# Last chunk of the last MLP: the left half of its columns from seven block products

## The chip, the cores and the metric

The kernel runs on one core of a Trainium2 chip. The metric is the device time of one execution in microseconds (us); for a kernel it is the median of several executions. A core has a matrix engine (TensorE, PE in the profile; its weight loads are PEld), a vector engine (VectorE, DVE), a scalar engine (ScalarE, ACT), GpSimd (POOL) and a queue engine (SyncE, SP). Each engine works through its own instructions in a fixed order and waits on semaphores that the others raise. DMA transfers are issued from SP, ACT or POOL and run on 16 DMA engines that they share.

## What is computed

A trunk of two layers over 256 tokens of width 2048: a state-space mixer in layer 0, a dilated attention mixer in layer 1, an MLP with squared ReLU behind each, and one last RMS norm. Only the second MLP and the norm behind it matter here:

```
def sq_relu_mlp(h, w1, w2):
    a = jax.nn.relu(h @ w1)
    return (a * a) @ w2

x = x + sq_relu_mlp(rms_norm(x, norm_mlp[i]), mlp_w1[i], mlp_w2[i])    # i = 1, the last layer
return rms_norm(x, final_norm)
```

`w1` is 2048 x 8192 and `w2` 8192 x 2048, all in float32.

## The kernel before

**Precision.** TensorE multiplies float32 in a fast format with a shorter mantissa (`F32R`). Each operand is therefore split in two: a high part, and a low part that holds the rest. For a unit of weights (128 x 2048 floats, 1 MB) ACT makes `wh` by a copy (`nc.scalar.activation(wh..)` in `fetch`), and DVE makes `wl` by subtracting `wh` from the weights. A product is then three matmuls: high by high, high by low, low by high.

**The plan.** `unit_plan` lists all units of weights in the order in which they are used, and `fetch` emits load and split of each, ahead of use. Units are numbered by their place in this list. A unit lands in one of three buffers `raw0` to `raw2` and is split into one of three or four slots of `wh` and `wl`; a slot is free once the matmuls of its last user are done. Chunks of the MLP may use four slots (`chunked`), plain units three.

**The MLP.** The 8192 hidden columns are cut into eight chunks of 1024 (`FC`). For chunk c, eight units of `w1` (`U0` to `U7`) give the hidden values, kept transposed in `r` (128 x 8 x 256: eight blocks of 128 hidden columns by 256 tokens). The chunk's part of `w2` is 1024 x 2048: eight units, each 512 hidden rows (half q) by 512 output columns (block j).

Chunks 0 to 6 do their part of `w2` by a seven-product scheme for 2 x 2 blocks (`PRODUCTS`, `PUT`, `Chunk.combine`, `product`). Blocks are the two halves of the hidden rows, the two halves of the tokens, and two neighbouring output blocks; the pair j = 0, 1 is marked `a` (left half of the columns) and the pair j = 2, 3 `b`. Each product has 12 matmuls of 128 x 512. On the side of the hidden values, `combine` forms the sums `s5`, `s6`, `s3`, `s7` on DVE and splits them. On the side of the weights, the sums are built up in place in a buffer `Aa` (or `Ab`):

- product 1 uses the block as it is loaded by SP;
- products 5 and 6 use `Aa` after another block was added to it by a transfer that POOL issues (`nc.gpsimd.dma_start(.., accum_op=ALU.add)`), the adding transfer;
- product 4 uses the negated sum of all four blocks. The fourth block is in `raw` for product 2 anyway, and DVE adds it (L263).

Products 3 and 7 use a second buffer `Ba` in the same way. An adding transfer into `Aa` can start only when the split of the value that is in it is done. The buffer `Aa` of a chunk is the same storage as `raw2` (`tag = f"raw{raws.use(2)}"` in `fetch`).

In `CHUNK_ORDER` the products of chunk c stand between the `w1` units of chunk c + 1: `1a U0 1b U1 5a U2 5b 3a ...`. Between products 1a and 5a TensorE works on U0, 1b and U1.

**The last chunk (c = 7)** has no next chunk, and all its eight units are plain (`rows_unit`): for each j, two units of 24 matmuls each (four blocks of hidden rows, two halves of the tokens, three matmuls), so 192 matmuls. `Chunk.complete` splits the one part of `r` that the plain form needs besides. After each j, DVE adds the result to `x_res` (`add_residual`) and `done(j)` runs, which is `gained` here: ACT squares the finished columns for the norm, and POOL multiplies them by the norm's gain `fin`. `fin` is loaded in `gained(0)`, into the buffer of `Ba`. For j = 3 both units are used together. After the last matmul stands a tail: the residual, the squares, the root, the scaling and the eight transfers to the output.

**What sets the order.** A scheduler orders each engine's instructions. The matmuls of a product are held behind those before them by `issue_after(latest[0])`, and the splits of the MLP's units are held in the order of the plan (`issue_after(high[i - 1])`, `issue_after(low[i - 1])`).

Of the kernel before, what the change touches and what calls it, by code (L numbers as in the profile page):

```python
# [8 lines left out]
F32 = mybir.dt.float32  # L9
# [5 lines left out]
P = 128  # L15
S = 256
NH = S // P
D = 2048
# [19 lines left out]
FC = 8  # L38
# [49 lines left out]

PRODUCTS = {
# [12 lines left out]
def mlp_plan(layer):  # L102
    plan = [("w1", layer, 0, u) for u in range(8)]
    for c in range(FC):
        if c + 1 < FC:
            for item in CHUNK_ORDER:
                if item[0] == "U":
                    plan.append(("w1", layer, c + 1, int(item[1])))
                else:
                    plan.append(("w2", layer, c, item))  # L110
        else:
            plan += [("w2", layer, c, j, q) for j in range(4) for q in range(2)]
    return plan
# [3 lines left out]
def hybrid_trunk_kernel(ctx: ExitStack, tc: tile.TileContext, a: dict, out: bass.AP):  # L117
    nc = tc.nc
# [24 lines left out]
    def bank(name, among):  # L143
        k = banks_of.use(banks_of.peek(among))
        return psum.tile([P, 512], F32, tag=f"b{k}", name=name, bufs=1)
# [24 lines left out]
    plan = unit_plan()  # L170
# [3 lines left out]
    latest = [None]  # L174
# [47 lines left out]
    def fetch(i, ends=(16,)):  # L222

        src, n = source(plan[i])
        kind = plan[i][0]
# [24 lines left out]
        ready[i] = (wh, wl)  # L250
        for k0, k1 in zip((0, *ends), ends):
            c = slice(k0 * n // 16, k1 * n // 16)
            if how == "load":
                load[i] = nc.sync.dma_start(raw[:, c], src[:, c]).ins
            elif how == "add" or kind == "wq":
                nc.gpsimd.dma_start(raw[:, c], src[:, c], accum_op=ALU.add)
            with ExitStack() as order:
# [3 lines left out]
                if item and item[0] == "2":  # L261
                    a = sums_of["A" + item[1]]
                    nc.vector.tensor_tensor(a[:, c], a[:, c], raw[:, c], ALU.add)  # L263
# [58 lines left out]
    def rows_unit(banks, us, lhs, k0, nk, n, first, last):  # L322

        ws = [take(*u) for u in us]
        kn = nk * len(us)
        for m in range(NH):
            t = slice(m * P, (m + 1) * P)
            for i in range(kn):
                wh, wl = ws[i // nk]
                c = slice((i % nk) * n, (i % nk + 1) * n)  # L330
                st, sp = first and i == 0, last and i == kn - 1
                hi, lo = lhs(k0 + i, 0, t), lhs(k0 + i, 1, t)
                nc.tensor.matmul(banks[m][:, :n], hi, wh[:, c], start=st, stop=False)  # L333
                nc.tensor.matmul(banks[m][:, :n], hi, wl[:, c], start=False, stop=False)  # L334
                latest[0] = nc.tensor.matmul(banks[m][:, :n], lo, wh[:, c], start=False, stop=sp).ins  # L335
# [710 lines left out]
    def mlp(layer, pool, xn, done):  # L1046
# [7 lines left out]

# [86 lines left out]
        for c in range(FC - 1):  # L1141
            of = cur.combine()
            nxt = Chunk(c + 1)
            for item in CHUNK_ORDER:
# [8 lines left out]
                kept = key == "za"  # L1153
                first = item[0] in "15" or item[0] == "2" and not (kept and c > 0)
# [3 lines left out]
                if not kept or c == FC - 2:  # L1158
                    j += 2 * (item[1] == "b")
                    xc = x_res[:, m, j * 512:(j + 1) * 512]  # L1160
                    nc.vector.tensor_tensor(xc, xc, banks[key], op)
            cur = nxt

# [21 lines left out]
    with tc.tile_pool(name="mlp1", bufs=1) as pool:  # L1185
# [5 lines left out]
        def gained(j):  # L1191
            if j == 0:
                fin.append(pool.tile([P, D], F32, tag="Ba", name="fin", bufs=1))
                nc.scalar.dma_start(fin[0], a["final_norm"].to_broadcast([P, D]))
# [5 lines left out]
            if j == 2:  # L1200
                nc.vector.tensor_reduce(mean[:, :, 0], ssq[:, :, :3], AX.X, ALU.add)
                nc.vector.tensor_scalar(mean[:, :, 0], mean[:, :, 0], 1.0 / D, EPS, ALU.mult, ALU.add)
# [110 lines left out]
```

## Time and profile before

| | us |
|---|---|
| median of three executions | 2531.31 (2530.99 to 2532.34) |
| the profiled execution | 2528.85 |
| its span, first to last instruction | 2527.1 |
| TensorE's wait before it starts the last chunk | 0 |
| from the start of the last matmul (2517.61) to the span's end | 9.49 |

The profile's page gives the busy time of each engine and the chain of work that ended last. Its other views list single instructions in order of time (start, duration, engine, line, output <- inputs, and in brackets how long the engine sat idle before it and what ended that), busy time by stretches of time, waits, and the DMA transfers with the time from issue to landing. TensorE is busy for 99% of the span. A matmul of 128 x 512 is listed with some 0.39 us, but the next one starts 0.227 us later: they overlap, so counts are multiplied by the distance of their starts.

### The profile page before, as it was taken

The page shows a single profiled execution, that of the slowest core. Times are in us where ns is not written, and L with a number is a line of the kernel's source. Part 1 is how long each engine was busy: PE and PEld are TensorE (multiplying, and loading weights), DVE is VectorE, ACT ScalarE, POOL GpSimd, SP SyncE. Part 2 cuts the span into 40 slices and gives each one's busy share as a digit, 9 for nine tenths or more (in the row PEclk, how much of TensorE's full clock was granted, in tenths as well). Part 3 has the DMA queues.
Part 4 walks back from the last instruction along what each step waited for, and adds up shares of the span by engine and source line. Part 5 has one row for each costly group of instructions (what it writes and reads, how often), then busy time and mean ns, then how long its engine had stood idle before and what let it go on. Part 6 is the DMA issues. An engine that isn't in the chain of part 4 may idle for free.

```text
span 2527.1 us, 34394 instructions
## 1 busy us (share of the span) xinstructions
PE 2508.9 (99%) x13737; PEld 2162.8 (86%) x13737; DVE 2057.1 (81%) x2287; ACT 1598.3 (63%) x1990; POOL 125.8 (5%) x143
## 2 busy tenths in 40 slices
PE   9999999999999999999999999999999999999998
PEld 7888888888888888888888999999888888888887
DVE  7778889798788889988886677677668989889885
ACT  7777677677666666666656666566566666666664
POOL 0001000100000000000000000000000000000001
PEclk9999999999999999999999999999999999999999
DMA  8557777877787899888955554444568988898883
GB/s 299 212 196 188 244 225 243 242 227 218 246 245 245 254 253 265 249 248 250 269 185 178 171 178 167 163 163 163 179 220 230 266 248 251 254 264 255 252 239 136
DMA packets 83696, 567.43 MB, mean 225 GB/s; under 512 B 9296, under 2 KB 9936, under 8 KB 20048
## 3 DMA queue, kind: packets, MB, share of 16 engines
q1 hardware_dynamic: 65232, 441.50, 47.8%
q0 software_dynamic: 15552, 113.25, 23.2%
q10 hardware_dynamic: 2752, 10.49, 1.2%
q8 instruction: 108, 1.77, 0.3%
q14 instruction: 52, 0.43, 0.0%
HBM read 563.04 MB, written 2.16 MB: 224 GB/s over the span
## 4 chain that ended last, share of the span: by engine, by line
PE 92%; DVE 2%; ACT 2%; DMA 1%; issue 1%; POOL 0%; SPq 0%; ACTq 0%; POOLq 0%; DVEq 0%
PE h L298 28%; PE qk L298 11%; PE c L298 7%; PE pxb L1130 6%; PE pxa L1130 6%; PE pwb L1130 3%; PE pwa L1130 3%; PE z L335 2%; PE z L333 2%; PE z L334 2%; PE v L333 2%; PE v L334 2%; PE v L335 2%; PE pzb L1130 2%; PE pza L1130 2%; DVE wl L271 1%
## 5 line engine op out<-in xcount | busy, mean ns | idle before, releaser
L271 DVE TENSOR_TENSOR wl<-raw,wh 128x2048 fp32r<-128x2048 f32 (+4 forms) x368 | 796.6, 2167 | 267.2 <-ACT wh L270 265.8
L270 ACT ACTIVATE wh<-raw 128x2048 fp32r<-128x2048 f32 (+4 forms) x368 | 669.5, 1821 | 357.3 <-PE h L298 78.2
L298 PE MATMUL h<-xn,wh 128*128 128x512 f32 x2048 | 690.2, 393 | 0.0
L298 PE MATMUL h<-xn,wl 128*128 128x256 f32 x2048 | 556.0, 281 | 0.2 <-DVE wl L271 0.2
L298 PEld LDWEIGHTS h<-xn,wh 128*128 128x128 f32 x2048 | 376.5, 188 | 75.4
L298 PEld LDWEIGHTS h<-xn,wl 128*128 128x128 f32 x2048 | 385.3, 188 | 14.3 <-DVE wl L271 0.5
L298 PE MATMUL c<-xn,wh 128*128 128x512 f32 x768 | 262.5, 394 | 1.5 <-ACT wh L270 1.4
L298 PE MATMUL qk<-xn,wh 128*128 128x512 f32 x768 | 259.3, 393 | 0.0
L298 PE MATMUL c<-xn,wl 128*128 128x256 f32 x768 | 210.7, 283 | 0.8 <-DVE wl L271 0.8
L298 PE MATMUL qk<-xn,wl 128*128 128x256 f32 x768 | 209.4, 284 | 0.0
L298 PEld LDWEIGHTS c<-xn,wh 128*128 128x128 f32 x768 | 142.0, 188 | 32.7 <-ACT wh L270 3.9
L298 PEld LDWEIGHTS qk<-xn,wh 128*128 128x128 f32 x768 | 141.2, 188 | 28.6
L298 PEld LDWEIGHTS c<-xn,wl 128*128 128x128 f32 x768 | 143.8, 188 | 5.6 <-DVE wl L271 1.8
L298 PEld LDWEIGHTS qk<-xn,wl 128*128 128x128 f32 x768 | 141.5, 188 | 3.6 <-issue 1.2
L270 ACT ACTIVATE wh<-Ab 128x2048 fp32r<-128x2048 f32 x42 | 80.4, 1915 | 81.6 <-DMA Ab<-in_w 54.8
L271 DVE TENSOR_TENSOR wl<-Ab,wh 128x2048 fp32r<-128x2048 f32 x42 | 96.1, 2288 | 18.6 <-ACT wh L270 18.4
L270 ACT ACTIVATE wh<-Aa 128x2048 fp32r<-128x2048 f32 x42 | 80.3, 1913 | 40.5 <-DMA Aa<-in_w 34.0
L271 DVE TENSOR_TENSOR wl<-Aa,wh 128x2048 fp32r<-128x2048 f32 x42 | 96.1, 2287 | 11.6 <-ACT wh L270 11.6
L1079 ACT ACTIVATE r<-r 128x256 f32<-128x256 f32 x128 | 52.2, 411 | 78.2 <-DVE r L1078 78.2
L333 PE MATMUL z<-wh,xn 128*128 128x512 f32 x256 | 98.7, 392 | 2.4 <-DVE c_5t L319 2.4
L335 PE MATMUL z<-wh,xn 128*128 128x512 f32 x256 | 100.1, 392 | 0.0
L334 PE MATMUL z<-wl,xn 128*128 128x512 f32 x256 | 99.9, 390 | 0.0
(471 smaller groups left out, 4967.7 us busy)
## 6 DMA issues: line engine op xcount, KB each, us to landing
raw<-in_w SPq DMA_DIRECT2D x172, 1024.0 KB, 5.5
raw<-in_w_in SPq DMA_DIRECT2D x74, 1024.0 KB, 4.9
raw<-in_w_qk SPq DMA_DIRECT2D x48, 1024.0 KB, 4.9
Aa<-in_w POOLq DMA_DIRECT2D x28, 1024.0 KB, 9.8
Ab<-in_w POOLq DMA_DIRECT2D x28, 1024.0 KB, 10.1
raw<-in_w_v SPq DMA_DIRECT2D x32, 768.0 KB, 4.4
A<-in_w_out POOLq DMA_DIRECT2D x18, 1024.0 KB, 9.0
raw<-in_w_out SPq DMA_DIRECT2D x14, 1024.0 KB, 7.6
```

What stands on the lines that cost most here:

```text
L270: high[i] = nc.scalar.activation(wh[:, c], raw[:, c], AF.Copy).ins
L271: low[i] = nc.vector.tensor_tensor(wl[:, c], raw[:, c], wh[:, c].bitcast(F32), ALU.subtract).ins
L298: latest[0] = nc.tensor.matmul(ps[:, :n], (wh, wl)[part][:, kt * P:(kt + 1) * P], xs[:, kt, :, :].rearrange("p a t -> p (a t)")[:, :n], st ...
L333: nc.tensor.matmul(banks[m][:, :n], hi, wh[:, c], start=st, stop=False)
L334: nc.tensor.matmul(banks[m][:, :n], hi, wl[:, c], start=False, stop=False)
L335: latest[0] = nc.tensor.matmul(banks[m][:, :n], lo, wh[:, c], start=False, stop=sp).ins
L1079: nc.scalar.activation(t, t, AF.Square)
L1130: latest[0] = nc.tensor.matmul(ps, lhs(i, part), w[:, n], start=(first and i == 0 and part == 0 and w is wh), stop=(i == 3 and part == 1), ...
```

## The change

The last chunk of the last MLP gets an order of its own, `LAST_ORDER`. Its left half (j = 0 and 1) comes from the seven products, and its right half (j = 2 and 3) stays plain: `P0`, `P1` are the two units of j = 2, set among the products, and `p0`, `p1` those of j = 3, at the end. In this chunk the fourth block is added to `Aa` by an adding transfer in place of DVE (`whole`), which reads that block a second time. `rows_unit` gets `strict`, which holds the second half of the tokens behind the first for j = 3. The norm's gain is loaded with j = 2, into the buffer of `Ab`, and j = 0 and 1 are finished after product 4a. The first MLP keeps its last chunk.

```diff
+LAST_ORDER = "1a 5a P0 3a 6a P1 7a 2a 4a p0 p1".split()
...
+        elif layer == 0:
+            plan += [("w2", layer, c, j, q) for j in range(4) for q in range(2)]
         else:
-            plan += [("w2", layer, c, j, q) for j in range(4) for q in range(2)]
+            plan += [("w2", layer, c, 2 + (item[0] == "p"), int(item[1])) if item[0] in "Pp" else
+                     ("w2", layer, c, item) for item in LAST_ORDER]
...
+        whole = kind == "w2" and plan[i][2] == FC - 1
...
-            elif how == "add" or kind == "wq":
+            elif how == "add" or kind == "wq" or how == "sum" and whole:
                 nc.gpsimd.dma_start(raw[:, c], src[:, c], accum_op=ALU.add)
...
-                if item and item[0] == "2":
+                if item and item[0] == "2" and not whole:
                     a = sums_of["A" + item[1]]
                     nc.vector.tensor_tensor(a[:, c], a[:, c], raw[:, c], ALU.add)
...
+            with ExitStack() as order:
+                if strict and m:
+                    order.enter_context(tc.issue_after(latest[0]))
...
-        for c in range(FC - 1):
+        last = FC - 1 if layer == 0 else FC
+        for c in range(last):
             of = cur.combine()
-            nxt = Chunk(c + 1)
-            for item in CHUNK_ORDER:
+            nxt = Chunk(c + 1) if c + 1 < FC else cur.complete()
+            for item in CHUNK_ORDER if c + 1 < FC else LAST_ORDER:
+                if item == "P0":
+                    plain = [bank(f"d{layer}_{c}_2_{m}", (0, 1)) for m in range(NH)]
+                if item[0] == "P":
+                    q = int(item[1])
+                    in_order(lambda: rows_unit(plain, [("w2", layer, c, 2, q)], cur.plain, 4 * q, 4, 512,
+                                               q == 0, q == 1))
+                    if q:
+                        add_residual(plain, 2)
+                        done(2)
+                    continue
+                if item == "p0":
+                    plain = [bank(f"d{layer}_{c}_3_{m}", (0, 1, 6)) for m in range(NH)]
+                    in_order(lambda: rows_unit(plain, [("w2", layer, c, 3, q) for q in range(2)], cur.plain,
+                                               0, 4, 512, True, True, strict=True))
+                    add_residual(plain, 3)
+                    done(3)
...
+                if c == FC - 1 and item == "4a":
+                    done(0)
+                    done(1)
...
-            if j == 0:
-                fin.append(pool.tile([P, D], F32, tag="Ba", name="fin", bufs=1))
+            if j == 2:
+                fin.append(pool.tile([P, D], F32, tag="Ab", name="fin", bufs=1))
...
-            if j == 2:
+            if j == 1:
                 nc.vector.tensor_reduce(mean[:, :, 0], ssq[:, :, :3], AX.X, ALU.add)
```

The units of the last chunk are numbered 551 to 558 before, and 551 to 561 with the change: 551 is 1a, 552 is 5a, 553 P0, 554 3a, 555 6a, 556 P1, 557 7a, 558 2a, 559 4a, 560 p0, 561 p1. Buffers carry the number of the unit for which they were first filled, so `Aa551` is the one buffer of 1a, 5a, 6a and 4a.

SP's queue at the end of the program, its last loads. Before:

```order
L254 DMA raw548_21110<-in_w1 128x2048
L254 DMA raw549_21129<-in_w2 128x2048
L254 DMA raw551_21167<-in_w2 128x2048
L254 DMA raw552_21213<-in_w2 128x2048
L254 DMA raw553_21250<-in_w2 128x2048
L254 DMA raw554_21280<-in_w2 128x2048
L254 DMA raw555_21320<-in_w2 128x2048
L254 DMA raw556_21350<-in_w2 128x2048
L254 DMA raw557_21388<-in_w2 128x2048
L254 DMA raw558_21418<-in_w2 128x2048
```

With the change:

```order
L262 DMA Ba554_21271<-in_w2 128x2048
L262 DMA raw548_21110<-in_w1 128x2048
L262 DMA raw549_21129<-in_w2 128x2048
L262 DMA Aa551_21166<-in_w2 128x2048
L262 DMA raw553_21265<-in_w2 128x2048
L262 DMA raw556_21311<-in_w2 128x2048
L262 DMA raw558_21359<-in_w2 128x2048
L262 DMA raw561_21434<-in_w2 128x2048
L262 DMA raw560_21415<-in_w2 128x2048
```

Eight plain loads become seven, and the load of 560 (p0) is issued last, behind that of 561 (p1). By the order of use of the three buffers, 553 takes `raw0`, 556 `raw1`, 558 `raw0`, 560 `raw2` and 561 `raw1`; `raw2` is the storage that `Aa551` holds until 4a is split.

POOL's queue at the end, the adding transfers and the norm's products (`x_res<-x_res,fin`). Before:

```order
L256 DMA Aa529_20515<-in_w2 128x2048
L256 DMA Ab531_20580<-in_w2 128x2048
L256 DMA Ba536_20751<-in_w2 128x2048
L256 DMA Bb538_20817<-in_w2 128x2048
L1199 TENSOR_TENSOR x_res_69<-x_res_69,fin_21312 128x512 x6
```

With the change:

```order
L264 DMA Ba536_20751<-in_w2 128x2048
L264 DMA Bb538_20817<-in_w2 128x2048
L264 DMA Aa551_21166<-in_w2 128x2048 x2
L264 DMA Ba554_21271<-in_w2 128x2048
L264 DMA Aa551_21166<-in_w2 128x2048
L1235 TENSOR_TENSOR x_res_69<-x_res_69,fin_21409 128x512 x6
```

Four adding transfers come in: three into `Aa551` (for 5a, 6a and 4a) and one into `Ba554` (for 7a).

DVE's instructions from the split of unit 550 (the last product of chunk 6) on; `h1_7_7` is the result of the last `w1` unit, `a21_7` and `a1r` are splits of the hidden values, `x_res<-x_res,p..` adds a product to the residual. Before:

```order
L266 SCALAR_TENSOR_TENSOR wl550_21150<-Ab531_20580,wh550_21149 128x2048
L271 TENSOR_TENSOR wl551_21169<-raw551_21167,wh551_21168 128x2048
L1082 TENSOR_TENSOR a21_7_20618<-r1_7_20619,a21_7_20618 128x256
L271 TENSOR_TENSOR wl552_21215<-raw552_21213,wh552_21214 128x2048
L319 TENSOR_TENSOR r1_7_20619<-h1_7_7_21166,h1_7_7x_21205 128x256
L1161 TENSOR_TENSOR x_res_69<-x_res_69,pzb1_6_21212 128x512
L1161 TENSOR_TENSOR x_res_69<-x_res_69,pxb1_6_20685 128x512
```

With the change (some rows on, `wl552` is the next split of weights):

```order
L274 SCALAR_TENSOR_TENSOR wl550_21149<-Ab531_20580,wh550_21148 128x2048
L279 TENSOR_TENSOR wl551_21168<-Aa551_21166,wh551_21167 128x2048
L1093 TENSOR_TENSOR a21_7_20618<-r1_7_20619,a21_7_20618 128x256
L327 TENSOR_TENSOR r1_7_20619<-h1_7_7_21165,h1_7_7x_21204 128x256
L1192 TENSOR_TENSOR x_res_69<-x_res_69,pzb1_6_21211 128x512
L1089 SCALAR_TENSOR_TENSOR r1_7_20619<-r1_7_20619,xn3rb_16307 128x256
L1192 TENSOR_TENSOR x_res_69<-x_res_69,pxb1_6_20685 128x512
L1122 TENSOR_TENSOR ssq_junk_75<-r1_7_20619 128x512
L1093 TENSOR_TENSOR a21_7_20618<-r1_7_20619,a21_7_20618 128x256
L1123 SCALAR_TENSOR_TENSOR s1_7_6_21243<-ssq_junk_75,r1_7_20619 128x512
L1117 TENSOR_TENSOR sp1_7_5_21248<-ssq_junk_75,sp1_7_5_21248 128x4x128
L1124 SCALAR_TENSOR_TENSOR s1_7_3_21244<-r1_7_20619,s1_7_6_21243 128x512
```

The split of unit 552, which stood two rows behind that of 551, now stands behind the sums of the hidden values (`ssq_junk`, `s`, `sp`). One row ahead of these stretches the add of `pza` of chunk 6 is gone; that product stays in its bank until 2a of the last chunk is added to it.

More of the change, by code (lines that the diff above doesn't have):

```diff
@@ L320, in cols_sum, with rows_unit @@
         return tot
-    def rows_unit(banks, us, lhs, k0, nk, n, first, last):
+    def rows_unit(banks, us, lhs, k0, nk, n, first, last, strict=False):
         ws = [take(*u) for u in us]
@@ L327, in rows_unit @@
             t = slice(m * P, (m + 1) * P)
[L328 to L335, printed above, removed]
+            with ExitStack() as order:
+                if strict and m:
+                    order.enter_context(tc.issue_after(latest[0]))
+                for i in range(kn):
+                    wh, wl = ws[i // nk]
+                    c = slice((i % nk) * n, (i % nk + 1) * n)
+                    st, sp = first and i == 0, last and i == kn - 1
+                    hi, lo = lhs(k0 + i, 0, t), lhs(k0 + i, 1, t)
+                    nc.tensor.matmul(banks[m][:, :n], hi, wh[:, c], start=st, stop=False)
+                    nc.tensor.matmul(banks[m][:, :n], hi, wl[:, c], start=False, stop=False)
+                    latest[0] = nc.tensor.matmul(banks[m][:, :n], lo, wh[:, c], start=False, stop=sp).ins
     def add_residual(banks, j):
@@ L1140, in mlp @@
         place = {"wa": 2, "wb": 3, "xa": 4, "xb": 5, "za": 7, "zb": 3}
-        for c in range(FC - 1):
+        last = FC - 1 if layer == 0 else FC
+        for c in range(last):
             of = cur.combine()
-            nxt = Chunk(c + 1)
-            for item in CHUNK_ORDER:
+            nxt = Chunk(c + 1) if c + 1 < FC else cur.complete()
[16 more added lines that the diff above has]
+                    done(3)
+                if item[0] == "p":
+                    continue
                 if item[0] == "U":
@@ L1153, in mlp @@
                 kept = key == "za"
+                out_now = not kept or c == last - 1
                 first = item[0] in "15" or item[0] == "2" and not (kept and c > 0)
@@ L1157, in mlp @@
                 product(c, item, banks[key], of[item[0]], first)
-                if not kept or c == FC - 2:
+                if out_now:
                     j += 2 * (item[1] == "b")
@@ L1161, in mlp @@
                     nc.vector.tensor_tensor(xc, xc, banks[key], op)
+                if c == FC - 1 and item == "4a":
+                    done(0)
+                    done(1)
             cur = nxt
+        if layer:
+            return
         c = FC - 1
```

## The prediction

> **What bounds the kernel now.** I read the page first: span, engines, and the chain of work that ended last.
>
> ```profile
> span 2527.1 us, 34394 instructions
> PE 2508.9 (99%) x13737; PEld 2162.8 (86%) x13737; DVE 2057.1 (81%) x2287; ACT 1598.3 (63%) x1990; POOL 125.8 (5%) x143
> PE 92%; DVE 2%; ACT 2%; DMA 1%; issue 1%; POOL 0%; SPq 0%; ACTq 0%; POOLq 0%; DVEq 0%
> ```
>
> TensorE is busy nearly always and makes up 92% of the chain. So a matmul less is time gained, but only as long as TensorE goes on without a wait. Next the stretches of the end (busy time and instructions of PE, PEld, DVE, ACT and POOL; granted clock; DMA share; GB/s):
>
> ```profile
> 2475.00:2500.00 25.00, 25.00 (x112) 20.73 (x111) 14.74 (x12) 12.84 (x15) 6.34 (x4) 1.00 0.47 175
> 2500.00:2518.00 18.00, 18.00 (x80) 14.58 (x78) 7.59 (x10) 5.43 (x9) 4.93 (x4) 1.00 0.07 25
> 2518.00:2520.00 2.00, 0.00 (x0) 0.00 (x0) 0.90 (x2) 0.72 (x2) 0.13 (x1) 1.00 0.84 305
> 2520.00:2523.00 3.00, 0.00 (x0) 0.00 (x0) 1.15 (x2) 1.33 (x2) 0.42 (x1) 0.95 0.41 151
> 2523.00:2527.00 4.00, 0.00 (x0) 0.00 (x0) 0.00 (x0) 0.00 (x0) 0.00 (x0) 0.50 0.41 151
> ```
>
> The last chunk (2475 to 2518) is matmuls without a gap, with DVE and ACT half idle and the DMA engines almost empty. So what the change takes from TensorE counts in full, and added work of DVE and ACT has room. What must be asked is whether weights come in time once they depend on each other.
>
> **What is removed.** Rows of the chain (start, duration, what):
>
> ```profile
> 2460.76 2.72 PE pxa L1130 x12
> 2463.48 5.55 PE h L298 x32
> 2469.03 2.73 PE pzb L1130 x12
> ```
>
> Twelve matmuls take 2.72 us, 0.227 each. Before, the last chunk has 192; now it has 7 x 12 + 4 x 24 = 180. The gain is 12 x 0.227 = **2.7 us**, 0.11%. No other edit shortens TensorE's path, so this is the most the change can give: less than the 0.2% (5 us) that a measurement of this kernel can tell from no change. DVE's add of the fourth block goes too, but DVE does not bound.
>
> **What is added: a chain of transfers.** The four values of `Aa551` follow each other in place: split for 1a, adding transfer, split for 5a, adding transfer, split for 6a, adding transfer, split for 4a. Chunk 6 shows one link of it, from the split for 1a to the split for 5a (DVE, POOL's issue, that one transfer's time from issue to landing, ACT, DVE):
>
> ```profile
> 2385.64 2.29 DVE L271 TENSOR_TENSOR wl<-Aa,wh 128x2048 fp32r<-128x2048 f32 x1
> 2388.22 0.86 POOL L256 DMA_DIRECT2D Aa<-in_w  x1 [48.66 <-DVE wl L271]
> DMA to landing us min/median/max: 8.6/8.6/8.6
> 2396.90 1.92 ACT L270 ACTIVATE wh<-Aa 128x2048 fp32r<-128x2048 f32 x1 [2.02 <-DMA Aa<-in_w]
> 2398.85 2.29 DVE L271 TENSOR_TENSOR wl<-Aa,wh 128x2048 fp32r<-128x2048 f32 x1 [0.26 <-ACT wh L270]
> ```
>
> Each piece starts when the one before it ends: a link is 2398.85 - 2385.64 = **13.2 us**. In chunk 6, U0, 1b and U1 (5.55 + 2.72 + 5.55 = 13.8 us by the rows above) stand on TensorE between 1a and 5a and cover it. In the last chunk 5a follows 1a at once: the cover is gone.
>
> Where the chain begins:
>
> ```profile
> 2465.33 0.68 DVE L1161 TENSOR_TENSOR x_res<-x_res,pza 128x512 f32<-128x512 f32 x1
> 2465.93 0.42 DVE L1078 SCALAR_TENSOR_TENSOR r<-r,xn3rb 128x256 f32<-128x256 f32 x1
> 2469.06 2.29 DVE L271 TENSOR_TENSOR wl<-raw,wh 128x2048 fp32r<-128x2048 f32 x1
> ```
>
> The last row is the split of unit 551. The add of `pza` ahead of it falls out (0.60 to the next start), so it starts at 2468.46.
>
> How long landings take: all 28 into `Aa`, and from chunk 6 one that another adding transfer overlaps from 4.3 us on (first issue and landing, then the second issue), and one that is issued while another is on its way (issue and landing).
>
> ```profile
> DMA to landing us min/median/max: 8.5/9.8/13.4
> 2410.85 0.88 POOL L256 DMA_DIRECT2D Ab<-in_w  x1 [8.56 <-DVE wl L271]
> DMA to landing us min/median/max: 9.2/9.2/9.2
> 2415.19 0.88 POOL L256 DMA_DIRECT2D Ba<-in_w  x1 [3.45 <-DVE wl L271]
> 2401.43 0.86 POOL L256 DMA_DIRECT2D Aa<-in_w  x1 [4.95 <-DVE wl L271]
> DMA to landing us min/median/max: 12.3/12.3/12.3
> ```
>
> The first and the third of the new transfers run beside plain loads alone: 8.6, as in the link shown. The second is overlapped by `Ba`'s about 4.5 us later, since `wl` of 553 and 554 come two splits behind that of 552: 9.2, so 0.6 more. The splits in the chain start at 2468.46 (551), 2481.67 (552), 2495.48 (555) and 2508.69 (559), and the last ends at 2510.98.
>
> **And one more link.** The load of 560 (p0) goes into the storage of `Aa551`, so it starts only then. Plain loads into `raw` from 2470 to 2492, landing:
>
> ```profile
> L254 SPq DMA_DIRECT2D raw<-in_w x5: 327/327/328, 2471.4 to 2489.7; - x5
> DMA to landing us min/median/max: 4.8/5.0/5.5
> ```
>
> Alone it takes 4.8: 2515.8. From the landing (2388.22 + 8.6 = 2396.82) to the start of `wl` the link has 2.0, then 2.3 for `wl`: 2520.1. p0's second matmul reads it. Loading 561 ahead of 560 saves nothing, since ACT, DVE and TensorE all take 560 first.
>
> **The sum.** The first matmul of 4b, the last product of chunk 6, starts here:
>
> ```profile
> 2471.60 0.39 PE L1130 MATMUL pxb<-wh,a 128*128 128x512 f32 x1
> ```
>
> With 4b and 1a, 24 matmuls, TensorE would be through 1a at 2477.0. Until p0's second matmul at 2520.1 it has 5a, P0, 3a, 6a, P1, 7a, 2a, 4a and one matmul, 121 x 0.227 = 27.5 us, in 43.1 us: it idles **15.6 us**. Behind it stand 47 matmuls, 10.7 us, to 2530.8. Before:
>
> ```profile
> 2517.61 0.39 PE L335 MATMUL d<-wh,a 128*128 128x512 f32 x1
> 2518.04 0.69 DVE L340 TENSOR_TENSOR x_res<-d,x_res 128x512 f32<-128x512 f32 x1 [1.40 <-PE d L335]
> ```
>
> There the last matmul's place ended at 2517.84. So the end moves by 2530.8 - 2517.8 = **+13.0 us**, which is 15.6 - 2.7. The tail behind the last matmul is the same work. The profiled execution (2528.85) would be 2541.8. The median of the runs shown is 2.5 above that execution, and a time is compared with medians, so I predict 2531.31 + 13.0 = **2544.3 us**.
>
> **What lies beside the chain.** Three more splits (ACT 1.92, DVE 2.29 each), and the sums and splits of the hidden values. From 4b's end (12 matmuls behind 2471.60: 2474.3) DVE has nine pieces of at most 0.69, 6 us, until 2480.3; `wl552` starts at 2481.67. They fit, with 1.4 to spare; with a landing below 7.2 us they would be late next. 3a, P0 and P1 wait for no adding transfer, but their splits are queued on ACT and DVE behind `wh552` and `wh555`, which wait: TensorE needs them a product later, so that costs nothing more. Two banks must be read by DVE before 7a and 4a add to them, and the reads stand behind splits of weights in DVE's order: about 1 us each of TensorE's idle time, inside the 15.6. 7a's transfer is issued by 2488.7 and, at `Ba`'s 11.4, lands by 2500; `wh557` is wanted after that. The gain `fin` (4.7 us, as before) now loads at about 2470, beside the first adding transfer, which the link shown had too (other loads). The squares and the four norm products of j = 0 and 1 move beside p0's matmuls: four times 0.82 on ACT, four times 1.3 to 2.8 on POOL, done by 2532 at worst; the root for the last tokens is wanted at 2532.6. Cost nothing to 0.5; I take nothing. `strict` only orders matmuls: nothing.
>
> For landings, the page "DMA: Bandwidth & Descriptors" of the Trainium skill (section on the anatomy of one DMA) fits a transfer issued by GpSimd as 2.0 us plus bytes over 436 GB/s, an estimate of 4.4 us for 1 MB. The 28 rows into `Aa`, from 8.5 up, disagree with it here, so the sum does not use it.
>
> **Rivals.**
>
> *A. The adding transfers are short where little else runs, and the change ends level or faster.* If one took what a plain load takes (4.8), a link would be 9.4. 552 would be split at 2480.2 (TensorE idle 2.9), 555 at 2489.6 (in time), 559 at 2499, and p0's weights would end at 2508.1, 1.0 after TensorE is free. Sum: 2.9 + 1.0 - 2.7 = +1.2, 2532.5; with landings fully hidden -2.7, 2528.6. The point of decision: three landings of 6.1 each bring the cost down to 5 us. For it: the DMA share is low there. Against it: no landing of 28 is under 8.5. By the skill's 4.4 above it would be this case. Chance 6%.
>
> *B. The load of 560 does not wait for the sum* (the change does not share the storage as I read it). Then p0 follows 4a, which can begin at about 2512.8 behind DVE's adds, and its 60 matmuls end at 2526.4: +8.6, 2539.9. Against it: three buffers are taken in turn and 560's turn is `raw2`. Chance 8%.
>
> *C. Landings collide.* The second, or all three, take 12.3 as in the last row above: +3.1 to +10.5 more, 2547.4 to 2554.8. For it: the DMA engines serve `Ba` and a load beside the second. Chance 13%.
>
> *D. The clock falls in a wait.* In the stretches above the granted clock is 1.00 until 2520, 0.95 over the next 3 us and 0.50 then: it halved at about 2522.7, 4.9 us after the last matmul. TensorE waits some 6.9 us before 5a's second matmul and some 4.6 before p0's, each with one matmul within. A slow start of 5a is hidden by the chain. Before p0 nothing hides it: between nothing and 47 x 0.227 = 10.7 us; 4.6 is just short of 4.9, so I take a fifth of it, 2: 2546.3. Chance 13%. The page "TensorE: Matmul & The Clock Gate" (what's actually happening) says that the clock halves after an idle window of about 3.4 us and is restored by as long a busy one; by it the price would be an estimate of 1.7 us. The halving agrees with the row; a return of the clock no run here shows.
>
> **How the numbers follow.** My own case, the chain with landings of 8 to 9.5, has 60% and spans 2541.5 to 2546. The range takes in B below and D and the one collided landing of C above: **2539.5 to 2550**. Slower by over 0.2% are my case, B, C and D: 0.94, of which I give 0.02 away for what I may have missed, so 0.92; within 0.2% 0.06; faster 0.02.
>
> **What would show it.** TensorE should idle until about 2483.9 for 5a, some 3 us before 6a, and until about 2520 for p0, with ACT waiting for the DMA into `Aa` each time, and SP's load of 560 issued right behind `wl559`. The four splits on DVE should start 13.2, 13.8 and 13.2 us apart. I am wrong if adding transfers land in under 6 us there, if 560's load is issued ahead of 4a's split, or if TensorE runs through.

## The result, and the profile after

| | before | with the change |
|---|---|---|
| median, us | 2531.15 (2530.80 to 2532.34, 4 runs) | 2546.91 (2545.53 to 2548.19, 4 runs) |
| ratio of the times | | 1.0061, 95% interval 1.0049 to 1.0073 |
| the profiled execution, us (its span) | 2528.85 (2527.1) | 2548.19 (2546.4) |

The kernel got slower by 15.8 us; the interval of the ratio makes that 12 to 18 us. The forecast was +13.0.

The page of the changed kernel: span, engines, and the chain of work that ended last.

```profile
span 2546.4 us, 34403 instructions
PE 2513.7 (99%) x13725; PEld 2163.3 (85%) x13725; DVE 2069.4 (81%) x2300; ACT 1607.2 (63%) x1997; POOL 128.1 (5%) x147
PE 90%; DVE 3%; DMA 3%; ACT 2%; issue 1%; POOL 0%; SPq 0%; ACTq 0%; POOLq 0%; DVEq 0%
```

TensorE has twelve matmuls less and is yet listed as busy for 4.8 us more (2513.7 against 2508.9): 2.8 of it lies in the last chunk, where matmuls that stand alone or run at a low clock count longer, and the rest far ahead of the change. Its share of the chain fell by 2 points, and DMA's rose by as much. Where that lies is seen in the order of time. The first matmul of 4b, from which the forecast counted, and DVE's last add into `x_res`, which follows the last matmul (start, duration, what):

```profile
2474.56 0.39 PE L1141 MATMUL pxb<-wh,a 128*128 128x512 f32 x1
2537.91 0.69 DVE L352 TENSOR_TENSOR x_res<-d,x_res 128x512 f32<-128x512 f32 x1 [1.85 <-PE d L347]
```

Before, the same two rows stood at 2471.60 and 2518.04. I call what lies between them **the stretch**: 46.44 us before, 63.35 now, so +16.9. It is the better measure in this case, since 4b starts 2.96 us later in this execution for reasons that lie hundreds of microseconds ahead of the change. The rest of the difference of the spans is the tail, which is 0.5 shorter (8.50 against 9.03, before rounding): 2.96 + 16.91 - 0.53 = 19.3.

The chain of waits through the last chunk, in order of time (the pieces that matter):

```profile
2474.01 9.58 DMA Aa<-in_w
...
2488.14 9.54 DMA Aa<-in_w
...
2502.45 9.32 DMA Aa<-in_w
...
2511.87 1.93 ACT wh L273
...
2513.82 2.30 DVE wl L274
...
2516.14 4.79 DMA raw<-in_w
...
2521.01 1.92 ACT wh L278
...
2522.95 2.30 DVE wl L279
...
2525.30 0.64 PE d L346
```

This is the serial chain: three adding transfers, the split of the sum of four, then the load of 560 into the storage that this split has just left, then its own split, then p0. TensorE appears in it only from p0's second matmul on, and there the next matmuls start 0.43 apart instead of 0.23. The four splits of `Aa551` on DVE show the links:

```profile
2471.43 2.29 DVE L279 TENSOR_TENSOR wl<-Aa,wh 128x2048 fp32r<-128x2048 f32 x1
2485.55 2.29 DVE L279 TENSOR_TENSOR wl<-Aa,wh 128x2048 fp32r<-128x2048 f32 x1 [2.84 <-ACT wh L278]
2499.72 2.29 DVE L279 TENSOR_TENSOR wl<-Aa,wh 128x2048 fp32r<-128x2048 f32 x1 [5.67 <-ACT wh L278]
2513.82 2.29 DVE L274 SCALAR_TENSOR_TENSOR wl<-Aa,wh 128x2048 fp32r<-128x2048 f32 x1 [2.56 <-ACT wh L273]
```

They start 14.1, 14.2 and 14.1 us apart; the forecast was 13.2, 13.8 and 13.2. TensorE's waits in the stretch, all of them (us in total, times, longest), where before there was none:

```profile
PE pwa L1141 <- ACT wh L278: 5.4, 1, 5.4
PE pxa L1141 <- DVE x_res L1192: 2.0, 2, 1.1
PE d L345 <- ACT wh L278: 1.9, 1, 1.9
PE d L346 <- DVE wl L279: 1.8, 1, 1.8
PE pwa L1141 <- DVE wl L279: 1.5, 1, 1.5
PE pxa L1141 <- DVE wl L279: 1.4, 1, 1.4
```

`pwa` is 5a, the rows `pxa` are 6a (1.4) and 7a and 4a (the two waits of 1 us for a bank to be read), and `d` is p0. And the granted clock around p0 (stretch of time; busy time and instructions of PE, PEld, DVE, ACT, POOL; clock; DMA share; GB/s):

```profile
2522.00:2526.00 4.00, 1.21 (x3) 0.78 (x4) 3.05 (x3) 3.40 (x5) 0.59 (x1) 0.94 0.00 0
2526.00:2530.00 4.00, 4.00 (x13) 3.10 (x13) 3.97 (x3) 2.10 (x6) 3.96 (x3) 0.63 0.00 0
2530.00:2537.00 7.00, 7.00 (x32) 5.80 (x31) 2.07 (x5) 2.06 (x4) 3.06 (x3) 1.00 0.10 39
```

The pause before p0 brought the clock down, and it was back by 2530. From p0's second matmul (2525.30) to the start of the last one (2537.48) there are 46 distances, 10.4 us at 0.227; it took 12.2, so **1.7 us** were lost to the clock.

So the profiled execution adds up: the forecast's 13.0, and 2.2 for links that are longer (42.4 in all against 40.2), and 1.7 for the clock, 16.9.

### The profile page after: what moved, and what is told of

The parts are those of the page before. It is cut to its first block, busy times and chain, and to the rows that moved or that the text cites. A ratio compares the mean times of both kernels' runs of the same rounds, so it can differ in the third digit from the quotient of the medians.

```text
span 2546.4 us, 34403 instructions
## 1 busy us (share of the span) xinstructions
PE 2513.7 (99%) x13725; PEld 2163.3 (85%) x13725; DVE 2069.4 (81%) x2300; ACT 1607.2 (63%) x1997; POOL 128.1 (5%) x147
## 4 chain that ended last, share of the span: by engine, by line
PE 90%; DVE 3%; DMA 3%; ACT 2%; issue 1%; POOL 0%; SPq 0%; ACTq 0%; POOLq 0%; DVEq 0%
PE h L306 28%; PE qk L306 11%; PE c L306 8%; PE pxa L1141 6%; PE pxb L1141 6%; PE pwb L1141 3%; PE pwa L1141 3%; PE z L347 2%; PE z L345 2%; PE z L346 2%; PE v L347 2%; PE v L345 2%; PE v L346 2%; DVE wl L279 2%; PE pzb L1141 1%; PE pza L1141 1%
## 5 line engine op out<-in xcount | busy, mean ns | idle before, releaser
L306 PEld LDWEIGHTS h<-xn,wl 128*128 128x128 f32 x2048 | 385.7, 188 | 14.2 <-DVE wl L279 0.5
L278 ACT ACTIVATE wh<-Aa 128x2048 fp32r<-128x2048 f32 x45 | 86.1, 1913 | 53.3 <-DMA Aa<-in_w 37.7
L279 DVE TENSOR_TENSOR wl<-Aa,wh 128x2048 fp32r<-128x2048 f32 x45 | 103.0, 2288 | 20.1 <-ACT wh L278 20.1
```

Source lines behind the costliest of these rows:

```text
L278: high[i] = nc.scalar.activation(wh[:, c], raw[:, c], AF.Copy).ins
L279: low[i] = nc.vector.tensor_tensor(wl[:, c], raw[:, c], wh[:, c].bitcast(F32), ALU.subtract).ins
L306: latest[0] = nc.tensor.matmul(ps[:, :n], (wh, wl)[part][:, kt * P:(kt + 1) * P], xs[:, kt, :, :].rearrange("p a t -> p (a t)")[:, :n], st ...
```

## The experiments

Theory T: the chain of split, adding transfer and split, with the load of 560 at its end, sets the time of the last chunk, and the clock adds to it. The rivals were that transfers cost because they collide, that the order of the matmuls alone costs, and that the clock alone does. Theory Q came up on the way: DVE's queue, in which reads of banks stand behind splits that wait.

All kernels are the changed one with one edit, and each was timed beside the kernel before on the same chip. The stretch is from each kernel's profiled execution. Two executions of the changed kernel differ by 0.8 in it, so a difference of less than 1 us is not taken for one.

| kernel | median, us | before there | ratio (95% interval) | stretch, us |
|---|---|---|---|---|
| before | | | | 46.4 |
| changed | 2546.91 | 2531.15 | 1.0061 (1.0049 to 1.0073) | 63.4 |
| changed, again | 2545.62 | 2529.81 | 1.0064 (1.0050 to 1.0078) | 62.5 |
| 1 own buffers for p0 and p1 | 2540.74 | 2529.24 | 1.0050 (1.0038 to 1.0062) | 59.0 |
| 2 fourth block added by DVE | 2548.15 | 2529.24 | 1.0070 (1.0057 to 1.0082) | 63.7 |
| 3 P0, P1 ahead of 5a, 6a | 2550.55 | 2529.24 | 1.0088 (1.0076 to 1.0100) | 69.5 |
| 4 matmuls in the pause | 2544.84 | 2529.24 | 1.0062 (1.0050 to 1.0074) | 61.7 |
| 5 no sums of weights | 2537.17 | 2529.81 | 1.0035 (1.0022 to 1.0048) | 54.8 |
| 6 gain's load in the gap | 2545.00 | 2529.40 | 1.0057 (1.0043 to 1.0070) | 61.0 |
| 7 order with cover | 2530.43 | 2529.81 | 1.0003 (0.9995 to 1.0012) | 47.1 |
| 8 the same, reads not placed | 2534.98 | 2529.81 | 1.0019 (1.0010 to 1.0028) | 52.1 |
| 9 order with cover, trimmed | 2530.96 | 2529.40 | 1.0009 (1.0000 to 1.0017) | 47.2 |

**The changed kernel once more.**

> The changed kernel itself once more, beside the kernel before on the same chip, so that the three runs after it have their own measure. All theories: about 15.8 us above the kernel before, ratio 1.006; the splits of 551, 552, 555 and 559 some 14 us apart; from the split of 551 to the add of the last tokens some 66.5 us (49.6 before).

+15.8 us again, on another chip. The links are 13.8, 13.2 and 14.5 us, 41.5 in all, and p0's matmuls lose 1.7 to the clock again: 13.0 + 1.3 + 1.7 = 16.0, and its stretch is 16.1 above that of before.

**1. Buffers of their own for p0 and p1.**

```diff
-            k = raws.use(raws.peek(range(2 if few(i) else 3)))
+            k = raws.use(raws.peek(range(2 if few(i) or plan[i][:4] == ("w2", 1, FC - 1, 3) else 3)))
```

> Only the buffers differ from the changed kernel: the loads of 560 and 561 (p0, p1) go into raw0 and raw1 and no longer wait for the split of the sum in Aa551. Theory T (a serial chain of split, adding transfer, split, and at its end the load of 560 into the same storage): the 4.8 us of that load leave the path, but the splits of 559 and 560 now follow each other at once on DVE, and the read of the bank that 4a adds to stands behind them, so about 2.3 us are gained by the wait; with it the pause before p0 is under 4 us and the granted clock there stays at 1.00, which is worth another 1.7: about 2543 (2541 to 2545), against 2547 for the changed kernel. Rival W (the load of 560 is covered, and what is late is the chain alone): no change, 2546 to 2548. Rival K (only the clock counts in that pause): 2545.2 with TensorE's waits before p0 as long as before.

The kernel is 11.5 us above before, where the changed one is 15.8 above: 4.3 less, and the stretch is 3.5 to 4.3 less. T's figure was 4.0. TensorE's waits now:

```profile
PE pwa L1141 <- ACT wh L278: 5.1, 1, 5.1
PE pxa L1141 <- DVE x_res L1192: 4.1, 2, 2.7
PE pwa L1141 <- DVE wl L279: 1.5, 1, 1.5
PE pxa L1141 <- DVE wl L279: 1.1, 1, 1.1
```

Both waits of p0 (`d`) are gone, and the clock is 1.00 through all of p0. But 7a and 4a wait longer for DVE to read their bank: half of the 4.8 us is handed on to DVE's queue, where the split of 560 now stands ahead of the last of these reads. So the shared storage costs about what T said, rival W falls, and a second queue is close behind.

**2. The fourth block added by DVE**, as in the other chunks.

```diff
-            elif how == "add" or kind == "wq" or how == "sum" and whole:
+            elif how == "add" or kind == "wq":
                 nc.gpsimd.dma_start(raw[:, c], src[:, c], accum_op=ALU.add)
...
-                if item and item[0] == "2" and not whole:
+                if item and item[0] == "2":
```

> One part undone: the fourth block is again added to Aa551 by DVE (about 2 us there), from the raw buffer that 2a uses, in place of the third adding transfer of about 9.5 us. Theory T by transfer time alone: the link from the split of 6a to that of 4a shrinks from 14.1 to about 7 us, and the time falls by up to 7: 2540. Theory T with queues: the add and its split stand on DVE behind the split for 2a, and the reads of banks behind these, and 560 still waits for the sum, so most of it is given back: 2543 to 2548. Rival C (landings that collide are what costs): one of the transfers that runs with 7a's goes, and the others get short, 2538 to 2541.

An adding transfer of 9.5 us goes, and nothing is gained: 18.9 above before, with an interval that holds the 15.8. The splits of the last four products on DVE (6a; 7a; 2a; 4a) show why:

```profile
2497.65 2.29 DVE L279 TENSOR_TENSOR wl<-Aa,wh 128x2048 fp32r<-128x2048 f32 x1 [4.86 <-ACT wh L278]
...
2504.84 2.29 DVE L279 TENSOR_TENSOR wl<-Ba,wh 128x2048 fp32r<-128x2048 f32 x1 [2.10 <-ACT wh L278]
2509.25 2.29 DVE L279 TENSOR_TENSOR wl<-raw,wh 128x2048 fp32r<-128x2048 f32 x1
2512.65 2.29 DVE L274 SCALAR_TENSOR_TENSOR wl<-Aa,wh 128x2048 fp32r<-128x2048 f32 x1
```

From 6a's split to 4a's it is still 15.0 us. The add starts at 2507.1, behind the split for 7a, which waits for its own transfer; then come the split for 2a and the reads. TensorE's new wait, 4.1 us before 7a, is for one of these reads. A shorter link was worth nothing here, since the engine that ends it was held by another wait.

**3. The plain units moved ahead of the products that wait.**

```diff
-LAST_ORDER = "1a 5a P0 3a 6a P1 7a 2a 4a p0 p1".split()
+LAST_ORDER = "1a P0 5a 3a P1 6a 7a 2a 4a p0 p1".split()
```

> The same parts in another order, 1a P0 5a 3a P1 6a 7a 2a 4a p0 p1: each of the plain units P0 and P1 (24 matmuls, 5.5 us) now stands before a product that waits for an adding transfer. Theory T (the chain of transfers on POOL and the splits between them set the end, and cover on TensorE only moves idle time about): TensorE's wait before 5a falls by some 5 us, but p0 starts no earlier, since splits are queued in the order of the plan and those of P0 and P1 now stand ahead of those for 5a and 6a: 2547 to 2551. Rival O (the order of matmuls costs it, 5a directly behind 1a without cover): 2536 to 2542.

21.3 above before, worse than the changed kernel by 5.5; T had allowed 16 to 20 (2547 to 2551 against 2531). Its profiled execution is the longest of its five, so the stretch counts for less here. The three longest entries among the waits:

```profile
PE pwa L1141 <- ACT sp L1116: 5.7, 1, 5.7
PE pxa L1141 <- DVE x_res L1192: 4.2, 2, 2.3
PE pwa L1141 <- DVE x_res L1192: 4.0, 1, 4.0
```

5a still waits, now for the split of its sum of hidden values (`sp`), which stands behind weights on ACT and DVE, and three waits are for banks to be read: T had left these out. The granted clock adds to them: over the stretch it was 0.83 on the mean, against 0.92 in the changed kernel. Moving the cover without looking at DVE's queue moved the waits. Rival O, by which this order would have gained 5 to 11 us, falls.

**4. Matmuls in the pause before p0.**

```diff
+                    warm_bank, line = bank("warmd", [5]), xs[:, 0, :, :].rearrange("p a t -> p (a t)")
+                    with tc.issue_after(latest[0]):
+                        for _ in range(18):
+                            latest[0] = nc.tensor.matmul(warm_bank, line[:, :P], line, start=True, stop=True,
+                                                         skip_group_check=True).ins
```

> 18 matmuls of 128 x 512 on old data into a free bank are added between 4a and p0, 4 to 7 us that fill TensorE's pause there; nothing reads the result. Clock theory (rival D of the prediction came true beside the chain: the pause lets the granted clock fall to half for p0's first matmuls, 1.7 us): they start 0.23 us apart from p0's first one on, and the time falls by about 1.7, to 2545; if the added matmuls outlast the pause, by less. Without a clock effect: 2547 to 2549.

Two of p0's first matmuls with the pause filled:

```profile
2521.21 0.40 PE L347 MATMUL d<-wh,a 128*128 128x512 f32 x1
2521.45 0.40 PE L345 MATMUL d<-wh,a 128*128 128x512 f32 x1
```

And two of the changed kernel's in its second execution, with the stretches of that execution (clock third from the end):

```profile
2522.65 0.63 PE L347 MATMUL d<-wh,a 128*128 128x512 f32 x1
2523.07 0.63 PE L345 MATMUL d<-wh,a 128*128 128x512 f32 x1
```

```profile
2520.00:2522.00 2.00, 1.36 (x6) 1.15 (x7) 2.00 (x3) 1.40 (x5) 1.25 (x1) 1.00 0.00 0
2522.00:2524.00 2.00, 2.00 (x7) 1.51 (x6) 2.00 (x1) 1.45 (x4) 1.97 (x2) 0.50 0.00 0
2524.00:2526.00 2.00, 2.00 (x8) 1.59 (x7) 1.32 (x3) 0.00 (x0) 2.00 (x2) 0.65 0.00 0
```

They start 0.24 us apart with the pause filled and 0.42 without, and with it filled the clock stays at 1.00 from 4a to the last matmul. So the pause causes the slow start. From p0's second matmul to the last it is 11.4 us against 12.2, not the 10.4 that the clock alone would give: p0's matmuls now come so fast that the split of 561 is late, a wait of 0.5. Of the 1.7 us only half came out, and the time cannot tell it from nothing (1.0062 against 1.0061 and 1.0064).

**5. No sums of weights in the last chunk.**

```diff
+        if item and plan[i][2] == FC - 1:
+            where, how = "raw", "load"
...
-            k = raws.use(raws.peek(range(2 if few(i) else 3)))
+            k = raws.use(raws.peek(range(2 if few(i) and not (kind == "w2" and plan[i][2] == FC - 1) else 3)))
```

> All four adding transfers leave the last chunk: 5a, 6a, 7a and 4a split blocks that SP loads plainly, each into a buffer in turn, so the sums of weights are left out of this chunk; matmuls, splits and their order stay. Theory T (the serial chain of split, adding transfer and split sets the end): only the wait before 5a is left, some 8 us, since the split of 552 stands behind the sums of hidden values on DVE; TensorE's last matmul comes about 8 us earlier than in the changed kernel, no wait before p0, about 7.5 us above the kernel before. Rival O (the order of the products alone is what costs, with 5a directly behind 1a): no change against the changed kernel, 15 to 16 us above the kernel before.

The kernel leaves the sums of weights out of this chunk. It is 7.4 us above before; T said 7.5. All waits that are left:

```profile
PE pwa L1143 <- ACT sp L1118: 5.2, 1, 5.2
PE pwa L1143 <- DVE sp L1119: 2.3, 1, 2.3
```

With the same number of matmuls in the same order, without the adding transfers, half of the cost is gone. The other half is the wait before 5a, and it is not one that the changed kernel has. The weights land early here, so two splits of them stand on DVE between the sum of hidden values that 5a needs (started at 2479.60) and its split. The second of these, and the split of the sum:

```profile
2483.34 2.29 DVE L281 TENSOR_TENSOR wl<-raw,wh 128x2048 fp32r<-128x2048 f32 x1
2485.55 0.68 DVE L1119 TENSOR_TENSOR sp<-ssq_junk,sp 128x512 fp32r<-128x512 f32 x1
```

In the changed kernel the same split ended at 2480.30, 3.3 us ahead of the first landing (2483.59). So the transfers cost at least the half that is gone. That the number agrees with T is in part luck. T had the queue the other way round, with 5a's split of weights behind the sums, and it left out the clock, which was 0.52 over 2482 to 2492. The stretch is 8.4 above before: 7.5 of waits and 3.5 of slow matmuls and restarts, less 2.7 for the twelve matmuls.

**6. The gain's load moved off the first transfer.** `fin` loads 1 MB, beside the first adding transfer.

```diff
-                nc.scalar.dma_start(fin[0], a["final_norm"].to_broadcast([P, D]))
+                with tc.issue_after(high[plan.index(("w2", 1, FC - 1, "5a"))]), tc.high_priority():
+                    nc.scalar.dma_start(fin[0], a["final_norm"].to_broadcast([P, D]))
```

> The changed kernel with one transfer moved: the load of the norm's gain fin (1 MB, issued by ACT 2 us ahead of the first adding transfer) is placed behind ACT's split of 552, so that it runs in the pause of some 4 us in which the DMA engines are idle. Theory S (an adding transfer lands later by what else the DMA engines carry meanwhile): the first landing falls from 8.8 to 9.6 us to 7.8 to 8.4, the first link by about 1 us and, since the whole chain sets the end, TensorE's end by as much, to about 1 us less than in the changed kernel; the second landing stays within 0.4 us. Rival V (landings differ from execution to execution, not by neighbours): the first landing stays at 8.8 to 9.6.

The three adding transfers in the chain of waits, and the stretches of the first one, which now runs alone:

```profile
2473.14 7.91 DMA Aa<-in_w
...
2485.60 8.88 DMA Aa<-in_w
...
2499.25 9.35 DMA Aa<-in_w
```

```profile
2476.00:2478.00 2.00, 2.00 (x10) 1.66 (x9) 1.38 (x3) 0.06 (x1) 0.00 (x0) 1.00 1.00 205
2478.00:2480.00 2.00, 1.30 (x6) 0.75 (x4) 2.00 (x5) 1.21 (x2) 0.00 (x0) 1.00 0.98 205
```

7.9 us alone, against 8.8 to 9.6 in the five executions (the changed kernel twice, runs 1, 2 and 4) that had the gain's load beside it: theory S, though from one execution without that load. By one adding transfer alone all 16 DMA engines are busy (0.98 to 1.00) while 205 GB/s move. In the kernel before, plain loads into `raw` from 2476 to 2478:

```profile
2476.00:2478.00 2.00, 2.00 (x11) 1.65 (x10) 1.08 (x1) 1.61 (x3) 0.00 (x0) 1.00 0.97 410
```

They fill them as well, but at 410 GB/s. So an adding transfer of 1 MB holds the DMA engines about twice as long as a load of the same size. The third transfer still takes 9.35, so its length does not come from the gain's load. The stretch is 1.5 us shorter than in the second execution of the changed kernel; the median (15.6 above before) can't tell it.

**7. An order with cover.** All four adding transfers stay. 4a comes last, so j = 0 is the norm's last column block; the plain units load into `raw0` and `raw1` alone, as p0 and p1 do in run 1; and DVE's reads of two banks are placed ahead of splits that wait.

```diff
-LAST_ORDER = "1a 5a P0 3a 6a P1 7a 2a 4a p0 p1".split()
+LAST_ORDER = "1a P0 P1 5a p0 3a 6a 2a 7a p1 4a".split()
+GATE = [('6a', '5a', 'p0'), ('7a', '6a', '2a')]
...
-            k = raws.use(raws.peek(range(2 if few(i) else 3)))
+            k = raws.use(raws.peek(range(2 if few(i) or plan[i][:3] == ("w2", 1, FC - 1) else 3)))
...
+                if i in gate:
+                    order.enter_context(tc.issue_after(reads[gate[i][0]]))
```

> The same products and the same four adding transfers in another order, 1a P0 P1 5a p0 3a 6a 2a 7a p1 4a, so that 24 to 48 matmuls of plain units stand between the links of the chain and 4a comes last; P and p units load into raw0 and raw1 alone; the norm's last column block is then j = 0; and on DVE the reads of the banks after 5a and after 6a are placed ahead of the splits for 6a and 7a. Theory T (the chain costs only where TensorE has nothing else to do, and 40 us of chain fit beside 43.6 us of matmuls): TensorE waits about 2 us before 7a and nowhere else, its last matmul comes some 15 us earlier than in the changed kernel, and the time is that of the kernel before, from 1 us below to 2 above (ratio 0.9995 to 1.001). Rival C (landings that collide set the cost, whatever the order): at least 5 us above the kernel before. Rival O2 (the seven products themselves cost on TensorE, by cold clock or pipeline breaks): 4 us above or more.

0.6 us above before, and no different from it. TensorE's waits:

```profile
PE pwa L1152 <- DVE sp L1128: 1.1, 1, 1.1
PE pxa L1152 <- DVE wl L284: 0.8, 1, 0.8
PE d L356 <- DVE wl L284: 0.3, 1, 0.3
```

The same transfers, with landings of 10.9, 8.4 and 10.3 (the sum of them is longer than in the changed kernel, since plain loads run beside), cost nothing more than these waits once 48 to 60 matmuls stand beside each link. So rival C falls: collisions are a term, not the cause. The waits of 2.2 us, and what a restart adds to them, use up the 2.7 us that the seven products save. The tail is 1.0 longer (10.0 from the last add to the span's end): ACT squares the last block 1.3 us after that add ends, behind its scaling of the other rows.

**8. The same order without the two placements on DVE.**

```diff
-GATE = [('6a', '5a', 'p0'), ('7a', '6a', '2a')]
...
-                if i in gate:
-                    order.enter_context(tc.issue_after(reads[gate[i][0]]))
```

> As the run before it, but without the two placements on DVE: the reads of the banks after 5a and 6a again stand behind the splits for 6a and 7a, which wait for adding transfers. Theory Q (a bank that the next product adds to is read too late, since DVE's queue is held by a split that waits): TensorE waits some 2.7 us before 3a and 3 us before 7a, released by DVE's add into x_res, and the time is about 3.6 us above that of the run with the placements. Rival: the same time within 1 us, as such reads fit in before.

4.6 us above the run with the placements; Q said 3.6, its rival none.

```profile
PE pwa L1142 <- DVE x_res L1192: 2.5, 1, 2.5
PE pxa L1142 <- ACT wh L273: 2.3, 1, 2.3
```

The first wait is 3a's, for DVE to read 5a's result. The second is 7a's; the profile names ACT, but ACT's `wh` there is for 4a, and DVE's read of the bank ended 0.14 ahead of 7a's first matmul: a wait for two things is put down to the later one by name, and here it is DVE again. Behind it the clock fell (0.53 over 2514 to 2517), which it did not in run 7; Q had not counted that.

With this run the three parts of run 7 can be told apart. Buffers of their own bring the kernel from 15.8 to 11.5 above before (run 1), the order, with the norm's new end, to 5.2 (this run), and the two placements to 0.6 (run 7).

**9. The same order, trimmed**: p1 in two halves around 7a, the fourth block added by DVE, the gain's load as in 6.

```diff
-LAST_ORDER = "1a P0 P1 5a p0 3a 6a 2a 7a p1 4a".split()
+LAST_ORDER = "1a P0 P1 5a p0 3a 6a 2a p1 7a p1- 4a".split()
```

> The order with cover once more, with its last waits taken out: p1 is cut in two halves of 12 matmuls, one ahead of 7a and one behind it, the fourth block is added by DVE again, and fin loads in the pause as in the run before it. Theory T: TensorE waits less than 2 us in all in the last chunk, and the time is 0 to 2 us below that of the kernel before, since at most 2.7 us of matmuls are saved: ratio 0.999 to 1.0005. Rival: a tail of its own takes the gain back, as j = 0 ends last now, and the ratio stays at 1.000 to 1.001.

It missed: 1.6 us above before, ratio 1.0009. The wait of 7a became one of p1, 2.3 us for its split, which now stands on DVE behind the add of the fourth block, and took 3.4 instead of 2.3 beside POOL's products. No version here is faster than the kernel before. At most 2.7 us were to be had, little more than the half-width of this interval (2.2 us).

## Why the prediction came out as it did

The time, 2546.9 us, lies in the range, but above the 2541.5 to 2546 of my own case. The two terms below on the links and the clock make the difference. None of the three signs of being wrong came: no adding transfer landed in under 6 us, the load of 560 came behind 4a's split, and TensorE waited.

- **What bounds, and the gain.** Right. TensorE ran without a wait before, and the twelve matmuls are worth their 2.7 us at most. Run 7, where little waits, ends level with the kernel before.
- **The chain and its cover.** Right, and shown from both sides: without the transfers at least half of the cost goes (5); with the same transfers, other matmuls beside them, buffers of their own and two reads placed ahead, all of it goes (7). Of these 15 us the order is worth some 6 (run 8 against run 1).
- **The load of 560.** Right: issued 0.03 after the split of the sum, 4.79 us to landing (4.8 forecast). Rival B, that it would not wait, is out; run 1 does what B describes. B's +8.6 was too low, though: run 1 measures +11.5, and its stretch is 4.0 above B's. Of that, 1.6 are longer links; 2.3 come from DVE's read ahead of 4a, which then stands behind the split of 560.
- **The size of a link.** This is the term that was too small: "The first and the third of the new transfers run beside plain loads alone: 8.6". They took 9.58 and 9.32, and the second 9.54 instead of 9.2. It made 2.2 us of the profiled stretch, 1.3 in the second execution. For the first transfer the step that failed is the one on `fin`, "which the link shown had too (other loads)": how much of a load lies inside the landing differs from case to case. In the link shown a load landed 2.5 us after the adding transfer was issued; here `fin` landed 3.6 us after, and run 6 shows 7.9 without it. For the third, "beside plain loads alone" failed: 7a's adding transfer landed at 2504.11, 1.7 us after the third was issued (2502.45). By the forecast's own times it had to overlap, as 6a's split at 2495.48 puts the third at about 2498.1 and `Ba` lands "by 2500". How much of the third's 9.32 is due to it and how much to the load of 561 beside it was not tried.
- **The clock.** Rival D was given 13% and came to pass beside my own case, not in its place: 1.7 us where "I take a fifth of it, 2". The estimate of 1.7 by the Trainium skill's page "TensorE: Matmul & The Clock Gate" (what's actually happening) is what the traces show. My reason to doubt it, a pause just short of 4.9 us "with one matmul within", did not hold: one matmul in the pause did not keep the clock up. Nor was 4.9 us, or the 3.4 us of the idle window that the forecast cites, a least length here: in the second execution a pause of 2.0 us before 7a was followed by 3.4 us at half clock (2508.3 to 2511.8), while in run 1 a pause of 2.8 us before 4a was followed by none. D should have been part of the sum.
- **Rival A** is out: alone a transfer takes 7.9, not the 6.1 from which A decides. "the DMA share is low there" was no reason for it, as one adding transfer brings that share to 1. A also leaves out DVE's queue, of which the forecast says that with a landing below 7.2 us its pieces "would be late next": in run 5, where weights land early, 5a waits 7.5 us, not A's 2.9. **Rival C**: no landing in `Aa` reached 12.3 in the changed kernel; in its two executions they were 0.7 to 1.8 us above the 7.9 of a transfer alone.
- **Beside the chain.** DVE's reads of two banks were forecast at about 1 us of waiting each and took 1.1 and 0.9. That they are next in line was not said; in runs 1, 2, 3 and 8 they are among the longest waits. Before 6a TensorE waited 1.4 us and not "some 3": after the pause before 5a its matmuls ran at half clock (0.58 over 2488 to 2492), which took up the rest, and the chain hid it, as the forecast said of a slow start of 5a.
- **The tail** was 0.5 us shorter, not the same.

What stays open: why landings of the same transfer beside the same load vary from 8.8 to 9.6 between executions, what lengthened the third, and how much of run 3's loss belongs to each of its waits.

## What to carry to other kernels

A transfer that adds in place makes a serial chain of everything that reads the buffer between the adds, and the next user of the storage is its last link: write the links down with their durations, and ask for each which matmuls stand beside it, before counting the matmuls saved. Then follow the queue of the engine that ends the links, here DVE: a short instruction behind a split that waits took the wait over here, and a shorter link brought nothing until it was placed ahead. And a pause on the busiest engine is priced with the slow start behind it.

## What the runs showed of the hardware

- An adding transfer of 1 MB took 7.9 us with nothing beside it (run 6), and held all 16 DMA engines at 0.98 to 1.00 while 205 GB/s moved; plain loads moved 410 GB/s at 0.97. With a load issued 2.0 us ahead of it, it landed after 8.8 to 9.6. Not every neighbour lengthens it: the second one in run 3 landed after 7.7, with another adding transfer issued 2.2 us behind it and a plain load 4.1 behind. Plain loads beside adding transfers landed after up to 12.3 us instead of 4.8 (run 3).
- DVE's split of 2.29 us took 3.08 to 3.38 while POOL ran its norm products (p1's split in the changed kernel and in runs 7 and 9).
- The clock can fall after the work has come back. In the second execution of the changed kernel TensorE paused from 2517.0 with one matmul at 2518.3, went on at 2520.6, ran 1.3 us at full clock, and then had half of it for 3.4 us (2522.0 to 2525.4, from the means of the stretches). In the first one the clock was low from about 2525.5 to 2528.9, 3.4 us again. In these two the fall came 4.6 and 5.0 us after the last matmul of 4a, ahead of the pause, and 0.2 and 1.3 us after work had come back; in all runs, where a pause ahead of a matmul was followed by a fall, it came 2.4 to 5.2 us after that last matmul. The Trainium skill's page "TensorE: Matmul & The Clock Gate" (what's actually happening) says that the clock is restored after a busy window of about 3.4 us. The 3.4 us here agree, and this is the return of the clock that no run showed at the time of the forecast.
